# Layer 1's norm weight and bias through the spatial product, plain fp32, and GpSimd's products on VectorE

## The chip, the core and the metric

The kernel runs on one core of a Trainium2 chip: TensorE does matmuls, VectorE and ScalarE elementwise work, GpSimd does elementwise work too, SyncE issues the transfers between HBM and SBUF. The metric is device time in microseconds, the median of several runs. The profile is one execution under the hardware profiler; its times are counted from the span's start.

## The reference

A trunk of two layers on 1024 tokens of width 1024. Layer 0 is a recurrence beside windowed attention and is not touched. Layer 1 is, cut to what matters:

```python
h = rms_norm(x, norm_c[j])
u, v, g = split_cols(h @ w_in_c[j], (2048, 2048, 2048))
v = layer_norm(v, ln_v_g[j], ln_v_b[j])          # (v - mean) * rstd * g + b, over the 2048 columns
# chunks of 128 tokens, 8 groups of 256 columns, W_s lower triangular, one per group
sg = einsum("gts,bcsgd->bctgd", w_s * causal, v) + b_s
y = u * sg * silu(g)
x = x + y @ w_out_c[j]
```

## The kernel before

All products are fp32 in three parts: each operand is split into a high part, a cast to fp32r on ScalarE, and a low part, the difference, made on VectorE, and `mm3` (lines 144 to 147) issues three matmuls. The large products use Winograd's scheme of quarters: seven products in place of eight.

Layer 1 first makes v (lines 956 to 1115) and stores it in HBM (`vdram`) by groups of 256 columns. Then comes the gating stage, lines 1117 to 1328: 8 groups, and in each a gate product and a u product, in this order (`order`, line 1152). Each has seven products of 4 x 3 matmuls of 512 columns (`group_product`, line 1230). After product i it evacuates an accumulator (`done`) and runs the steps listed for i. The order of all engines' work is written out by hand there, and each engine takes its instructions strictly in that order. The steps are these:

- `group_operands` (line 1118) loads the raw weights of the product after next in two tiles (pool of two) and makes, during the running product, the four operands of the next one: sums on GpSimd (`add_up`, line 1134), splits on ScalarE and VectorE (`split`, lines 1141 and 1142), at steps 0 to 3, 5 and 6.
- `group_prep` (line 1195) loads v of the group, its norm weight and bias, the spatial bias and weights, at the start of the gate product; `group_mask` (line 1208, GpSimd) and `group_ws` (line 1212, TensorE transpose and split) run at steps 4 and 5 of it.
- `group_norm` (line 1220) normalizes one token tile of 256 columns of v in two VectorE steps and splits it; its eight calls lie in the steps of the u product.
- `group_u` (line 1259) adds up the quarters of u and multiplies them by the gate, three of four on GpSimd (line 1272).
- `group_spatial` (line 1277) is called four times per group, in steps 0 to 3 of the next gate product: eight matmuls against W's two parts side by side, two additions per bank on VectorE (lines 1292 and 1294), the product with u on GpSimd (line 1295), a store to `ydram`.

An accumulator of a product is reused by a later one: product 3 needs the copy that `done(0)` makes on ScalarE, product 5 that of `done(2)`, product 7 the addition of `done(4)` on VectorE (counted from 1). PSUM has 8 banks that are given out in turn; SBUF has 16 large tiles, of which 14 hold the token operands here and the other two v and the gate of a group.

After the stage the output projection (`winograd`, line 709) loads y back from `ydram` (`load_y`), makes its sums on GpSimd (`combine`, line 748) and splits on ScalarE and VectorE. There the order on ScalarE and VectorE is a planner's.

Of the kernel before, what the change touches and what calls it, by code (L numbers as in the profile page):

```python
# [18 lines left out]
P = 128  # L19
# [8 lines left out]
# the weights to split in a step of mixer B's chunk, by their place in the order of use  # L28
# [8 lines left out]
R_CONV_W, R_CONV_B, R_GAB, R_GXB, R_LAM = 0, 32, 40, 48, 56  # L37
N_ROWS = 64


def bc(ap, pos, n):
    """The access pattern with a repeated dimension of n inserted at pos."""
    dims = [list(d) for d in ap.ap]
    dims.insert(pos, [0, n])
    return bass.AP(tensor=ap.tensor, offset=ap.offset, ap=dims)


def flip(ap):
    """The access pattern with its innermost dimension read backwards."""
# [6 lines left out]
def rows_bc(ap, n):  # L56
    """A DRAM row of n elements, repeated over the partitions."""
    return bass.AP(tensor=ap.tensor, offset=ap.offset, ap=[[0, P], [1, n]])
# [3 lines left out]
def trunk_kernel(  # L62
# [58 lines left out]
    def fetch_weights(i):  # L121
        """Start the loads of the weights up to i, as far as they have not been started."""
# [4 lines left out]
    def load_weights(i, prefetch=True):  # L127
        """Split the weights up to i, as far as they have not been split."""
# [30 lines left out]
    def power_rsqrt(dst, mean, width, name):  # L159
        """dst = (mean + EPS) ** -0.5 on a few columns."""  # L160
# [7 lines left out]
    def norm_rs(xt, t, pool):  # L168
        """The scratch tile of the scaled rows and their reciprocal root mean square."""
# [14 lines left out]
    def h_tiles(tag):  # L184
        """[feature half][token half] tiles of 4 x 512, high and low parts."""
# [24 lines left out]
    # =================== layer 0: norm, keys, values, first gate ===================  # L210
# [35 lines left out]
    # keys of a head: [k; k] stacked over partitions, high and low parts;  # L246
    # values of a block and head: [high | low | high]
# [3 lines left out]
    def kv_pass(t, w_part, h_part, first, last):  # L251
        """One of the three products of parts of the normed rows with the keys' and values' weights."""
# [55 lines left out]
    def load_consts():  # L308
# [3 lines left out]
        for r0, src in ((R_CONV_B, conv_b), (R_GAB, gate_a_b), (R_GXB, gate_x_b), (R_LAM, lru_lambda)):  # L312
            nc.sync.dma_start(out=rows[r0:r0 + 8, :], in_=src[0].rearrange("(k p) -> k p", p=P))
        nc.sync.dma_start(out=rows[R_CONV_W:R_CONV_W + 32, :],
                          in_=conv_w[0].rearrange("w (k p) -> (w k) p", p=P))

    def tail_consts():
        """What is needed later on: the bias by distance, through DRAM for its skewed read, and mixer A's columns."""
# [1088 lines left out]
```

## Time and profile before

| | us |
|---|---|
| median of 3 runs | 1453.38 (1451.16 to 1453.53) |
| span of the profiled execution | 1451.4 |
| TensorE matmuls busy | 1348.5 (93%) |
| VectorE busy | 1111.1 (77%) |
| ScalarE busy | 693.9 (48%) |
| GpSimd busy | 506.3 (35%) |

How to read it: a busy share is an average over stages with different limits, and matmuls overlap in the pipeline, so that a TensorE that is busy is not one without gaps. The distance between the starts of two matmuls says what one costs.

### The profile page before, as it was taken

The page shows a single profiled execution, that of the slowest core. Times are in us where ns is not written, and L with a number is a line of the kernel's source. Part 1 is how long each engine was busy: PE and PEld are TensorE (multiplying, and loading weights), DVE is VectorE, ACT ScalarE, POOL GpSimd, SP SyncE. Part 2 cuts the span into 40 slices and gives each one's busy share as a digit, 9 for nine tenths or more (in the row PEclk, how much of TensorE's full clock was granted, in tenths as well). Part 3 has the DMA queues.
Part 4 walks back from the last instruction along what each step waited for, and adds up shares of the span by engine and source line. Part 5 has one row for each costly group of instructions (what it writes and reads, how often), then busy time and mean ns, then how long its engine had stood idle before and what let it go on. Part 6 is the DMA issues. An engine that isn't in the chain of part 4 may idle for free.

```text
span 1451.4 us, 18932 instructions
## 1 busy us (share of the span) xinstructions
PE 1348.5 (93%) x7003; PEld 1148.9 (79%) x7003; DVE 1111.1 (77%) x1830; ACT 693.9 (48%) x1282; POOL 506.3 (35%) x350
## 2 busy tenths in 40 slices
PE   7999999999999996599998799999988998997998
PEld 6888888888887785488888799777777777775887
DVE  6468888888788889778678745778877887879873
ACT  6467878776777763134423223333333333432430
POOL 3322333221032339300035232444455444488100
PEclk9999999999999998799999899999999999999999
DMA  6212111112211054014412123233223322683321
GB/s 208 59 30 58 29 46 30 44 32 71 58 33 51 4 188 174 16 44 146 159 37 80 68 93 135 65 113 113 91 65 117 109 91 66 216 334 132 113 96 64
DMA packets 100536, 133.53 MB, mean 92 GB/s; under 512 B 5355, under 2 KB 72028, under 8 KB 98396
## 3 DMA queue, kind: packets, MB, share of 16 engines
q1 hardware_dynamic: 100444, 132.32, 27.1%
q8 instruction: 55, 0.90, 0.3%
q14 instruction: 37, 0.30, 0.1%
HBM read 107.11 MB, written 25.19 MB: 91 GB/s over the span
## 4 chain that ended last, share of the span: by engine, by line
PE 59%; DVE 22%; issue 8%; POOL 4%; ACT 4%; DMA 3%; SPq 0%; DVEq 0%; POOLq 0%; ACTq 0%
PE m L145 6%; PE m L146 5%; PE m L147 5%; DVE wlg L1142 3%; PE v L145 3%; PE v L146 3%; PE v L147 3%; DVE wl_w L696 2%; DVE wa L689 2%; PE pq L145 2%; PE gb L145 2%; PE pq L147 2%; PE gb L147 2%; PE pq L146 2%; PE gb L146 2%
## 5 line engine op out<-in xcount | busy, mean ns | idle before, releaser
L145 PE MATMUL m<-wh_w,wa 128*128 128x512 f32 x432 | 170.8, 395 | 34.0 <-DVE x L824 34.0
L146 PE MATMUL m<-wl_w,wa 128*128 128x512 f32 x432 | 170.5, 395 | 4.2 <-DVE wl_w L696 4.2
L147 PE MATMUL m<-wh_w,wa 128*128 128x512 f32 x432 | 170.0, 393 | 0.0
L145 PEld LDWEIGHTS m<-wh_w,wa 128*128 128x128 f32 x432 | 82.3, 190 | 52.9 <-issue 32.8
L146 PEld LDWEIGHTS m<-wl_w,wa 128*128 128x128 f32 x432 | 82.3, 190 | 21.6 <-DVE wl_w L696 5.0
L147 PEld LDWEIGHTS m<-wh_w,wa 128*128 128x128 f32 x432 | 82.3, 190 | 17.3
L1226 ACT CAST vh<-vg 128x256 fp32r<-128x256 f32 x64 | 26.0, 407 | 122.3 <-DVE vg L1224 122.3
L530 DVE CUSTOM_DVE_ANT_0 e<-ps,e,sink_bc 128x256 f32<-128x256 f32 (+1 forms) x128 | 62.3, 525 | 20.6 <-PE ps L527 20.2
L600 POOL TENSOR_TENSOR yb<-ot,yb 128x256 f32<-128x256 f32 x32 | 23.6, 736 | 144.9 <-DVE ot L598 127.2
L134 DVE TENSOR_TENSOR wl<-raw,wh 128x1024 fp32r<-128x1024 f32 x38 | 49.4, 1307 | 26.4 <-ACT wh L133 26.2
L1295 POOL TENSOR_TENSOR ug<-yt,ug 128x512 f32<-128x512 f32 x32 | 41.9, 1319 | 71.5 <-DVE yt L1294 71.4
L696 DVE TENSOR_TENSOR wl_w<-b,wh_w 128x1024 fp32r<-128x1024 f32 x36 | 60.7, 1693 | 6.8 <-ACT wh_w L695 6.8
L545 ACT ACTIVATE e<-e,nm 128x256 f32<-128x256 f32 (+1 forms) x128 | 61.6, 486 | 0.4 <-DVE nm L535 0.4
L695 ACT CAST wh_w<-b 128x1024 fp32r<-128x1024 f32 x36 | 37.5, 1046 | 46.9 <-DVE b L748 22.7
L1272 POOL TENSOR_TENSOR ug<-ug,sg 128x512 f32<-128x512 f32 x24 | 40.7, 1699 | 51.0 <-DVE ug L1271 51.0
L824 DVE TENSOR_TENSOR x<-m,x 128x512 f32<-128x512 f32 x56 | 37.4, 684 | 24.9 <-PE m L147 24.7
L902 POOL TENSOR_TENSOR ya<-ya,r 128x1024 f32<-128x1024 f32 x8 | 22.9, 2859 | 91.2 <-DVE r L898 65.5
L145 PE MATMUL pq<-hh,wh 128*128 128x512 f32 x128 | 52.5, 410 | 0.0
L145 PE MATMUL ga<-hh,wh 128*128 128x512 f32 x128 | 50.3, 393 | 2.2 <-DVE ya L867 2.2
L145 PE MATMUL gb<-hh,wh 128*128 128x512 f32 x128 | 50.3, 393 | 0.0
L145 PE MATMUL za<-hh,wh 128*128 128x512 f32 x128 | 50.2, 392 | 0.0
L147 PE MATMUL pq<-hh,wl 128*128 128x512 f32 x128 | 50.2, 392 | 0.0
(405 smaller groups left out, 4619.0 us busy)
## 6 DMA issues: line engine op xcount, KB each, us to landing
raw<-in_w_in_a_dram SPq DMA_DIRECT2D x34, 512.0 KB, 4.1
b<-in_w_out_a_dram SPq DMA_DIRECT2D x22, 512.0 KB, 6.9
b<-in_w_out_c_dram SPq DMA_DIRECT2D x22, 512.0 KB, 6.0
rawg<-in_w_in_c_dram SPq DMA_DIRECT2D x16, 512.0 KB, 3.6
rawu<-in_w_in_c_dram SPq DMA_DIRECT2D x16, 512.0 KB, 3.7
vg<-vdram SPq DMA_DIRECT2D x8, 1024.0 KB, 5.8
ydram<-ug SPq DMA_DIRECT2D x32, 256.0 KB, 2.4
yg<-ydram SPq DMA_DIRECT2D x8, 1024.0 KB, 10.8
```

Of the source, the lines that this page charges most:

```text
L134: nc.vector.tensor_tensor(out=lo, in0=raws[j], in1=hi.bitcast(F32), op=ALU.subtract)
L145: nc.tensor.matmul(acc, lhsT=lh, rhs=rh, start=first, stop=False, skip_group_check=shared)
L146: nc.tensor.matmul(acc, lhsT=lh, rhs=rl, start=False, stop=False, skip_group_check=shared)
L147: nc.tensor.matmul(acc, lhsT=ll, rhs=rh, start=False, stop=last, skip_group_check=shared)
L530: nc.vector.tensor_tensor_reduce(out=e[:, h, k0:256], in0=acc[:, j * 256:j * 256 + kw], in1=e[:, h, k0:256], scale=rs[:, 2 * (b % 4) + j:2 ...
L545: nc.scalar.activation(out=e[:, h], in_=e[:, h], func=AF.Exp, bias=st["nm"][:, h:h + 1], accum_out=st["sums"][:, h:h + 1])
L695: nc.scalar.copy(out=hi, in_=src)
L696: nc.vector.tensor_tensor(out=lo, in0=src, in1=hi.bitcast(F32), op=ALU.subtract)
L824: nc.vector.tensor_tensor(out=dst, in0=accs[m], in1=dst, op=add)
L1142: nc.vector.tensor_tensor(out=lo[:, j], in0=src, in1=hi[:, j].bitcast(F32), op=ALU.subtract)
L1272: nc.gpsimd.tensor_tensor(out=us[j], in0=us[j], in1=gates[j], op=ALU.mult)
L1295: nc.gpsimd.tensor_tensor(out=ug, in0=y.rearrange("p c t -> p (c t)"), in1=ug, op=ALU.mult)
```

## The change

The layer norm's mean and scale stay with v, as one ScalarE activation per token tile (`rstd` times v plus `shift`). Its weight and bias move behind the spatial product: since that product runs over tokens and the two run over columns, y = weight x (W_s v) + (bias x row sum of W_s + b_s). The last term is `offset`, made once with a matmul of ones. The spatial weights of all groups are loaded, masked and transposed once, in the first gate product. Nothing is split: v and W_s go into TensorE as plain fp32, four matmuls of 128 columns per call in place of eight of 256. One bank per call in place of two, one fused VectorE step in place of four additions. Weight and bias reach the partitions as columns of `cols`, by two more small loads and a longer transpose at the kernel's start. v's tile is read by TensorE itself now, and so the load of the next group's v stands at step 4 of the gate product. The weight sums (`add_up`), the products with the gate and the products with u move from GpSimd to VectorE.

```diff
-R_CONV_W, R_CONV_B, R_GAB, R_GXB, R_LAM = 0, 32, 40, 48, 56
-N_ROWS = 64
+R_CONV_W, R_CONV_B, R_GAB, R_GXB, R_LAM, R_LNG, R_LNB = 0, 32, 40, 48, 56, 64, 80
+N_ROWS = 96
...
         for r0, src in ((R_CONV_B, conv_b), (R_GAB, gate_a_b), (R_GXB, gate_x_b), (R_LAM, lru_lambda)):
             nc.sync.dma_start(out=rows[r0:r0 + 8, :], in_=src[0].rearrange("(k p) -> k p", p=P))
+        for r0, src in ((R_LNG, ln_v_g), (R_LNB, ln_v_b)):
+            nc.sync.dma_start(out=rows[r0:r0 + 16, :], in_=src[0].rearrange("(k p) -> k p", p=P))
         nc.sync.dma_start(out=rows[R_CONV_W:R_CONV_W + 32, :],
                           in_=conv_w[0].rearrange("w (k p) -> (w k) p", p=P))
...
@@ -1131,7 +1133,7 @@
             sums.append(late["vp"].tile([P, 4, P], F32, tag="sum", name=f"s{i}{kind}{g}", bufs=4))
             p, q, op = ((a21, a22, ALU.add), (sums[0], a11, ALU.subtract), (a11, a21, ALU.subtract),
                         (a12, sums[1 % len(sums)], ALU.subtract))[i]
-            nc.gpsimd.tensor_tensor(out=sums[i], in0=p, in1=q, op=op)
+            nc.vector.tensor_tensor(out=sums[i], in0=p, in1=q, op=op)
...
     rstd = const.tile([P, NT], F32, name="rstd")
     for t in range(NT):
         nc.vector.bn_aggr(out=mv[:, t, :], in_=st_all[:, t].rearrange("p a b -> p (a b)"))
+    shift = const.tile([P, NT], F32, name="shift")
     power_rsqrt(rstd, (mv[:, :, 1], 1.0), NT, "lnm")
-    def group_prep(g):
-        v = big_tile(F32, f"vg{g}").rearrange("p (t c) -> p t c", t=NT)
-        nc.sync.dma_start(out=v, in_=vdram[g])
-        lng = gp.tile([P, 256], F32, tag="lng", name=f"lng{g}")
-        lnb = gp.tile([P, 256], F32, tag="lnb", name=f"lnb{g}")
-        sb = gp.tile([P, P], F32, tag="sb", name=f"sb{g}", bufs=2)
-        nc.sync.dma_start(out=lng, in_=rows_bc(ln_v_g[0, g * 256:(g + 1) * 256], 256))
-        nc.sync.dma_start(out=lnb, in_=rows_bc(ln_v_b[0, g * 256:(g + 1) * 256], 256))
-        nc.sync.dma_start(out=sb, in_=rows_bc(spatial_b[0, g], P))
-        ws = gp.tile([P, P], F32, tag="ws", name=f"ws{g}")
-        nc.sync.dma_start(out=ws, in_=spatial_w[0, g])
-        return v, lng, lnb, sb, ws
-    def group_mask(ws):
-        nc.gpsimd.affine_select(out=ws, in_=ws, pattern=[[-1, P]], compare_op=ALU.is_ge, fill=0.0, base=0,
-                                channel_multiplier=1)
-    def group_ws(g, ws):
-        pt = bank(f"pw{g}")
-        nc.tensor.transpose(pt[:, :P], ws, ident)
-        w2 = gp.tile([P, 2, P], F32R, tag="w2", name=f"w2{g}")
-        nc.scalar.copy(out=w2[:, 0, :], in_=pt[:, :P])
-        nc.vector.tensor_tensor(out=w2[:, 1, :], in0=pt[:, :P], in1=w2[:, 0, :].bitcast(F32), op=ALU.subtract)
-        return w2.rearrange("p r t -> p (r t)")
-    def group_norm(t, v, lng, lnb, vh, vl, eng):
-        vv = v[:, t, :]
-        nc.vector.scalar_tensor_tensor(out=vv, in0=vv, scalar=mv[:, t, 0:1], in1=lng,
-                                       op0=ALU.subtract, op1=ALU.mult)
-        nc.vector.scalar_tensor_tensor(out=vv, in0=vv, scalar=rstd[:, t:t + 1], in1=lnb,
-                                       op0=ALU.mult, op1=ALU.add)
-        nc.scalar.copy(out=vh[:, t, :], in_=vv)
-        for i in [t - 1] * (t > 0) + [t] * (t == NT - 1):
-            eng.tensor_tensor(out=vl[:, i, :], in0=v[:, i, :], in1=vh[:, i, :].bitcast(F32), op=ALU.subtract)
+    nc.vector.scalar_tensor_tensor(out=shift, in0=mv[:, :, 0], scalar=-1.0, in1=rstd, op0=ALU.mult, op1=ALU.mult)
+    ws_raw = gp.tile([P, 8, P], F32, name="ws_raw")
+    sb_all = gp.tile([P, 8 * P], F32, name="sb_all")
+    ws_t = gp.tile([P, 8, P], F32, name="ws_t")
+    offset = gp.tile([P, 16, P], F32, name="offset")
+    ones = gp.tile([P, P], F32, name="ones")
+    nc.sync.dma_start(out=ws_raw, in_=spatial_w[0].rearrange("g t s -> t g s"))
+    nc.sync.dma_start(out=sb_all, in_=rows_bc(spatial_b[0, 0], 8 * P))
+    nc.vector.memset(ones, 1.0)
+    def spatial_mask():
+        nc.gpsimd.affine_select(out=ws_raw, in_=ws_raw, pattern=[[0, 8], [-1, P]], compare_op=ALU.is_ge, fill=0.0,
+                                base=0, channel_multiplier=1)
+    def spatial_transpose(i):
+        pt = bank(f"pw{i}")
+        for j in range(4):
+            nc.tensor.transpose(pt[:, j * P:(j + 1) * P], ws_raw[:, 4 * i + j, :], ident)
+        nc.scalar.copy(out=ws_t[:, 4 * i:4 * i + 4, :], in_=pt.rearrange("p (g t) -> p g t", g=4))
+    def spatial_offset(i):
+        pr = bank(f"rw{i}")
+        nc.tensor.matmul(pr, lhsT=ones, rhs=ws_t[:, 4 * i:4 * i + 4, :].rearrange("p g t -> p (g t)"), start=True,
+                         stop=True)
+        for j in range(8):
+            g = 4 * i + j // 2
+            nc.vector.scalar_tensor_tensor(out=offset[:, 8 * i + j, :], in0=pr[:, (j // 2) * P:(j // 2 + 1) * P],
+                                           scalar=col(R_LNB, 8 * i + j), in1=sb_all[:, g * P:(g + 1) * P],
+                                           op0=ALU.mult, op1=ALU.add)
+    vgs = {}
+    def load_v(g):
+        vgs[g] = big_tile(F32, f"vg{g}").rearrange("p (t c) -> p t c", t=NT)
+        nc.sync.dma_start(out=vgs[g], in_=vdram[g])
+    def group_norm(t, g):
+        vv = vgs[g][:, t, :]
+        nc.scalar.activation(out=vv, in_=vv, func=AF.Identity, scale=rstd[:, t:t + 1], bias=shift[:, t:t + 1])
...
                 nc.vector.tensor_tensor(out=us[j], in0=acc, in1=us[j], op=ALU.add)
-                nc.gpsimd.tensor_tensor(out=us[j], in0=us[j], in1=gates[j], op=ALU.mult)
+                nc.vector.tensor_tensor(out=us[j], in0=us[j], in1=gates[j], op=ALU.mult)
...
-    def group_spatial(g, d, half, ug, vhl, w2, sb):
-        vh, vl = vhl
+    def group_spatial(g, d, half, ug):
         y = gp.tile([P, 4, P], F32, tag="yt", name=f"yt{g}_{d}_{half}", bufs=2)
-        avs, yys = [], []
-        for i in range(2):
-            acc = bank(f"s{g}_{d}_{half}_{i}")
-            for j in range(2):
-                ch = half * 4 + i * 2 + j
-                o = acc[:, j * 256:(j + 1) * 256]
-                nc.tensor.matmul(o, lhsT=vh[:, ch, d * P:(d + 1) * P], rhs=w2, start=True, stop=False)
-                nc.tensor.matmul(o, lhsT=vl[:, ch, d * P:(d + 1) * P], rhs=w2, start=False, stop=True)
-            avs.append(acc.rearrange("p (c r t) -> p r c t", c=2, r=2))
-            yys.append(y[:, 2 * i:2 * i + 2, :])
-        for av, yy in zip(avs, yys):
-            nc.vector.tensor_tensor(out=yy, in0=av[:, 0], in1=bc(sb, 1, 2), op=ALU.add)
-        for av, yy in zip(avs, yys):
-            nc.vector.tensor_tensor(out=yy, in0=av[:, 1], in1=yy, op=ALU.add)
-        nc.gpsimd.tensor_tensor(out=ug, in0=y.rearrange("p c t -> p (c t)"), in1=ug, op=ALU.mult)
+        acc = bank(f"s{g}_{d}_{half}")
+        for i in range(4):
+            nc.tensor.matmul(acc[:, i * P:(i + 1) * P], lhsT=vgs[g][:, half * 4 + i, d * P:(d + 1) * P],
+                             rhs=ws_t[:, g, :], start=True, stop=True)
+        nc.vector.scalar_tensor_tensor(out=y, in0=acc.rearrange("p (c t) -> p c t", c=4), scalar=col(R_LNG, 2 * g + d),
+                                       in1=bc(offset[:, 2 * g + d, :], 1, 4), op0=ALU.mult, op1=ALU.add)
+        nc.vector.tensor_tensor(out=ug, in0=y.rearrange("p c t -> p (c t)"), in1=ug, op=ALU.mult)
         nc.sync.dma_start(out=ydram[g, :, d, half * 512:(half + 1) * 512], in_=ug)
...
     spatial = []
+    load_v(0)
     for n, (kind, g) in enumerate(order):
         nxt, steps = following
         if kind == "g":
-            v, lng, lnb, sb, ws = group_prep(g)
-            w2 = []
             for i, args in enumerate(spatial):
                 steps.setdefault(i, []).insert(i > 0, (group_spatial, *args))
-            steps.setdefault(4, []).append((group_mask, ws))
-            steps[5].append((lambda: w2.append(group_ws(g, ws)),))
+            if g == 0:
+                steps.setdefault(2, []).append((spatial_mask,))
+                for i in range(2):
+                    steps.setdefault(4 + i, []).append((spatial_transpose, i))
+            else:
+                steps.setdefault(4, []).append((load_v, g))
             sg = group_gate(g, ops, steps)
         else:
-            vh = gp.tile([P, NT, 256], F32R, tag="vh", name=f"vh{g}")
-            vl = gp.tile([P, NT, 256], F32R, tag="vl", name=f"vl{g}")
             for i in range(8):
-                steps.setdefault(i // 2 if g == 7 else min(i, 6), []).append(
-                    (group_norm, i, v, lng, lnb, vh, vl, nc.gpsimd if g == 7 else nc.vector))
+                steps.setdefault(i // 2 if g == 7 else min(i, 6), []).append((group_norm, i, g))
+            if g == 0:
+                for i in range(2):
+                    steps.setdefault(2 + 2 * i, []).append((spatial_offset, i))
             us = group_u(g, ops, sg, steps)
-            spatial = [(g, d, half, us[2 * d + half], (vh, vl), w2[0], sb)
-                       for d, half in ((0, 0), (0, 1), (1, 1), (1, 0))]
+            spatial = [(g, d, half, us[2 * d + half]) for d, half in ((0, 0), (0, 1), (1, 1), (1, 0))]
```

## Rows read from the trace of the kernel before

**Rows 1.** The page: busy time of the engines, and the chain by engine.

```profile
PE 1348.5 (93%) x7003; PEld 1148.9 (79%) x7003; DVE 1111.1 (77%) x1830; ACT 693.9 (48%) x1282; POOL 506.3 (35%) x350
...
PE 59%; DVE 22%; issue 8%; POOL 4%; ACT 4%; DMA 3%; SPq 0%; DVEq 0%; POOLq 0%; ACTq 0%
```

**Rows 2.** Timeline of TensorE, the gating stage's ends (start, us, instruction).

```profile
898.95 0.40 PE L145 MATMUL g<-gh,whg 128*128 128x512 f32 x1
...
1283.64 0.47 PE L145 MATMUL m<-wh_w,first_c 128*128 128x512 f32 x1 [2.33 <-DVE yt L1294]
```

**Rows 3.** Timeline of TensorE, a stretch without a stop and the stop behind it.

```profile
1068.46 0.39 PE L145 MATMUL u<-t1h,whu 128*128 128x512 f32 x1
...
1073.67 0.39 PE L147 MATMUL u<-t0h,wlu 128*128 128x512 f32 x1
1076.15 0.50 PE L145 MATMUL u<-t2h,whu 128*128 128x512 f32 x1 [2.09 <-ACT ug L1266]
```

**Rows 4.** Timeline of TensorE, one call of the spatial product.

```profile
1087.75 0.28 PE L1287 MATMUL s<-w,vh 128*128 128x256 f32 x1
...
1088.71 0.39 PE L145 MATMUL g<-gh,whg 128*128 128x512 f32 x1
```

**Rows 5.** Waits from 895 to 1290 (total us, times, longest).

```profile
PE u L145 <- ACT ug L1266: 16.2, 11, 2.3
...
PE pw L1214 <- POOL ws L1209: 9.0, 7, 1.3
...
PE m L145 <- DVE yt L1294: 2.3, 1, 2.3
```

**Rows 6.** Timelines of VectorE and ScalarE ahead of the stop in rows 3.

```profile
1069.33 3.01 DVE L1142 TENSOR_TENSOR wlg<-rawg,whg 128x512 fp32r<-128x512 f32 x2
...
1075.21 0.40 ACT L1226 CAST vh<-vg 128x256 fp32r<-128x256 f32 x1 [5.93 <-DVE vg L1224]
1075.52 0.58 ACT L1266 COPY ug<-u 128x512 f32<-128x512 f32 x1
```

**Rows 7.** Groups by line and shape, 930 to 1290 (busy, mean ns).

```profile
L1142 DVE TENSOR_TENSOR wlu<-s0u,whu 128x512 fp32r<-128x512 f32 x7 | 12.4, 1774 | 0.0
...
L1142 DVE TENSOR_TENSOR wlg<-s1g,whg 128x512 fp32r<-128x512 f32 x7 | 4.8, 692 | 8.0 <-ACT whg L1141 8.0
```

**Rows 8.** Busy times (PE, PEld, DVE, ACT, POOL) of 48 us inside the stage.

```profile
1045.00:1093.00 48.00, 43.77 (x201) 35.41 (x201) 38.30 (x63) 16.48 (x33) 22.33 (x16) 1.00 0.28 95
```

**Rows 9.** Transfers by line (KB each, median us from issue to landing).

```profile
rawu<-in_w_in_c_dram SPq DMA_DIRECT2D x16, 512.0 KB, 3.7
vg<-vdram SPq DMA_DIRECT2D x8, 1024.0 KB, 5.8
```

**Rows 10.** fp32 matmuls: two lines (ns min/median/max), and TensorE's timeline around them.

```profile
L484 PE MATMUL st<-pair_ones,sq x128: 171/251/252, 79.2 to 314.8; 128*128 128x2 f32 x128
...
79.22 0.95 PE L484 MATMUL st<-pair_ones,sq 128*128 128x2 f32 x8
80.04 0.48 PE L145 MATMUL pq<-hh,wh 128*128 128x512 f32 x1
...
L320 PE MATMUL pb<-oh,rel_ext x2: 482/488/493, 28.2 to 28.5; 33*16 33x384 f32 x2
...
28.18 0.82 PE L320 MATMUL pb<-oh,rel_ext 33*16 33x384 f32 x2
```

**Rows 11.** A fused VectorE step with a scalar per partition, line 181 (ns min/median/max).

```profile
L181 DVE SCALAR_TENSOR_TENSOR nxs<-xp,nrs,gain_a x10: 744/1270/1285, 8.5 to 40.7; 128x1024 f32<-128x1024 f32 x6, 128x512 f32<-128x512 f32 x4
```

**Rows 12.** Timeline of SyncE's queue: the raw weights' two halves, the second waiting.

```profile
1074.92 15.47 SPq L1125 DMA_DIRECT2D rawu<-in_w_in_c_dram  x2
```

**Rows 13.** Timelines of SyncE's queue and ScalarE at the kernel's start.

```profile
17.89 1.02 SPq L125 DMA_DIRECT2D raw<-in_w_in_a_dram  x2
...
26.58 1.04 ACT L133 CAST wh<-raw 128x1024 fp32r<-128x1024 f32 x1
```

**Rows 14.** Timeline of TensorE in the output projection.

```profile
1334.87 0.77 PE L145 MATMUL m<-wh_w,wa 128*128 128x512 f32 x1 [7.42 <-DVE x L824]
```

## Prediction, before the change was run

> **What bounds the kernel now.** I began with the busy times and the chain of work that ended last [rows 1]: TensorE is busy 93% of the span and carries 59% of the chain, VectorE 22%. That makes TensorE the engine to watch, but not the cause of every microsecond. So I went to the stretch that the change touches, the gating stage, from the first matmul of its first gate product at 898.95 to the first matmul of the output projection at 1283.64 [rows 2]: 384.7 us.
>
> How much of that is work? Between two matmuls of 512 columns without a stop lie (1073.67 - 1068.46) / 23 = 0.2265 us [rows 3]. The stage has 16 products of 7 x 4 x 3 = 84 such matmuls: 1344 x 0.2265 = 304.4. The spatial products are 256 matmuls of 256 columns, eight from 1087.75 to 1088.71, so 0.12 each [rows 4]: 30.7. With eight small transposes, some 0.6 in all, that makes 335.7, so 49.0 us of the stage are not work. That is the most which this stage can give if TensorE's work stays the same.
>
> The list of waits says where the 49.0 are [rows 5]: TensorE waits 16.2 for ScalarE's copy of a u quarter, 9.0 for GpSimd's mask of the spatial weights and 2.3 at the end for VectorE's `yt`: 27.5. The other 21.5 I put down to smaller waits and to what stands right behind each stop (weight loads that wait too, and matmuls that start slower). Who is at the root? One stop read backwards [rows 6]: TensorE stands until 1076.15 [rows 3]; ScalarE's copy began at 1075.52, behind a cast that had waited 5.93 us for VectorE's norm; ahead of that norm VectorE had taken 3.01 us for two subtractions. Undisturbed, such a subtraction takes 0.692 us; of the groups that run beside GpSimd's work one takes 1.774 [rows 7]. So GpSimd's products slow VectorE, VectorE's norm holds ScalarE, and ScalarE holds TensorE. VectorE itself is busy 38.3 of 48 us, GpSimd 22.3 [rows 8].
>
> **The change, part by part.**
>
> *The norm.* Per token tile two VectorE steps, a cast and a subtraction go; one ScalarE activation with scale and bias per partition comes, 64 in all, while 64 casts of 0.40 us go. Nearest row for it: that cast; I take 0.40 and bound it by 0.40 and the 0.58 of a copy of twice the columns [rows 6]. It waits for the load of v alone. That load moves from the start of a gate product to its fifth step, since the tile is now read by the spatial matmuls until the fourth. It issues after TensorE's fourth product and the four stores of `ydram`, by my count 17 us into the product, lands 5.8 us later [rows 9] at 22.8, and is wanted when u's first product is done, near 25.3. If it were over 2.5 us later, ScalarE's queue would hold the copies of u behind it.
>
> *The spatial product in plain fp32.* Eight matmuls become four. The records show two passes for each fp32 matmul: the line of query statistics has 128 for 64 matmuls in the code [rows 10]. Two prices: a pass bound by its weights takes (80.04 - 79.22) / 8 = 0.102; for one bound by streaming, two records of 384 columns that last 0.48 each end 0.82 after the first began, so they start 0.34 apart, 0.88 ns per column, 0.113 for 128 [rows 10]. I take 0.112 as these overlap for other matmuls: 256 passes, 28.7 us in place of 30.7. Bounds: 0.102 (26.1) and load plus stream, 0.215 (55.0). The Trainium skill (FP8 and Floating Point Precision, TensorE Precision Notes) says that a true fp32 product goes through the array four times; with four passes, each with its load, at 0.112 us the 128 matmuls would take 57.3, and the sum below would be 28.6 higher.
>
> *Mask and transposes.* Eight masks and eight transposes inside the loop become one mask and eight transposes in the first gate product: the 9.0 us wait goes. New on TensorE are two fp32 matmuls of 512 columns for the offset: 2 x 2 x 512 x 0.88 ns = 1.8 us, and 8 x 0.11 = 0.9 for the transposes. On VectorE come 16 steps of 128 columns in the first u product, some 4 us (estimate, between a quarter of 0.69 each, 2.8, and the whole, 11), for which it has a third of that product free, some 6 us; what is beyond that stands in the 5 us left over below. The mask is the only GpSimd work; it starts when `ws_raw` has landed, two products ahead of the transposes. The step `shift` makes VectorE wait once for a GpSimd power on 8 columns, while TensorE has 19 us of product ahead; I count nothing.
>
> *GpSimd's products go to VectorE.* Per pair of products (gate and u) VectorE then has 14 subtractions, 8 weight sums, 6 additions, 1 + 3 products with the gate, 4 products with u and 4 fused steps: 36 x 0.69 + 4 x 0.75 = 27.8 us (0.75: the shortest fused step, one of 512 columns [rows 11]). Now it is 38.3 in 48 [rows 8]. Nothing slows it any longer, and the pair shrinks to 38.1 + 3.6 = 41.7 us of TensorE: VectorE would be 67% busy. Queue order matters more: the first weight sum waits in VectorE's queue for the second half of the raw weights, and behind it stand the addition of product 2 and all later ones. These weights are issued when the last split of the product before is done. Now that is late for u (1090.39, 5.4 us into the gate product, as 1074.92 + 15.47; the product began near 1085.0, 12 x 0.2265 ahead of the spatial matmul at 1087.75 [rows 4, 12]); with no backlog I expect 1.8 us, plus 3.7 of transfer [rows 9]: 5.5 us into a product of 19 to 22.6. From there to the addition that product 7 needs lie 11.3 us of VectorE's work in a gate product, done at 16.8; product 7 starts at 19.9. In u it is 7.7 us, or 0.7 us behind product 5; either way before 16.3. So it is covered, by about 2 to 3 us.
>
> *The ends.* Two more small loads stand on SP's queue ahead of the raw weights at 17.89; two issues there take 1.02 us; were it three times that, the weights would issue near 21 and, with 3.7 of transfer, land near 24.7. They are first split at 26.58 [rows 13]: that cover holds, and the cost is 0. Without it, it would be some 1 to 3 us. At the other end the stop of 2.3 us for `yt` goes (already counted), and GpSimd can begin the output projection's sums some 5 us sooner against TensorE, since its products with u no longer stand before them. TensorE stops there once for 7.42 us behind VectorE [rows 14], which GpSimd slows in the same way. I take 2 us, between 0 and 5.
>
> *Sum.* Work after: 304.4 + 28.7 + 0.9 + 1.8 = 335.8. Of the 49.0 I leave 5 (estimate: small losses at 64 changes between the two kinds of products, and the crowded first pair). Stage: 340.8, a gain of 43.9; with the ends 45.9. The profiled execution spans 1451.4 and the median is 1453.4, 2.0 more: 1451.4 - 45.9 + 2.0 = **1407 us**.
>
> **Rivals.** (1) *VectorE late by a little.* It is the only engine for all elementwise steps and strictly in order. If raw weights land 9.6 instead of 5.5 us into a product, the cover of about 3 us is gone and each of the 16 products loses about 1 us: 1407 + 16 = 1423. For it: VectorE's tail is long today and rawu lands near 9.1 us into a gate product (5.4 + 3.7). Against it: that lateness comes from work that is removed.
> (2) *fp32 costs more.* If load and stream of a pass don't overlap, or each matmul has four loaded passes: 55.0 to 57.3 in place of 28.7, so 1407 + 26 to 29, say 1435. Against it: 128 records for 64 matmuls, at 0.102 us each. The Trainium skill's rule of four passes, cited above, would end there.
> (3) *Slower than before.* The same queue, but as a loop: a late last split delays the raw weights, these delay all of VectorE's steps, and these delay the next split. It decides from a landing 11.4 us into every product: 8.6 us is where product 7 begins to wait (19.9 - 11.3, or 16.3 - 7.7), and 44 / 16 = 2.8 us more per product eat the whole gain. At 12.5 us: 1453 + 18 = 1471. For it: a wait for a DMA at the head of the busiest queue. Against it: transfers of 3.6 to 3.7 us and a VectorE with a third of its time free.
> (4) *The gain is given back.* The output projection is short of VectorE; if its stops grow by 8 us, or its order of VectorE's work comes out worse, 1415.
>
> **How the numbers follow.** Forecast 0.62, rival 1 0.17, rival 2 0.10, rival 4 0.05, rival 3 0.06 (of which a third lands near no change). The low end takes the forecast with nothing left of the 49.0, 5 us at the end and the cheap pass: 1407 - 5 - 3 - 2.6, about 1397. The high end takes in rivals 1 and 4 and a few us more: 1427. Out of it stay rivals 2 and 3, 16 in 100. Faster by over 0.2% (what a measurement of this kernel can tell from none): 0.94; within: 0.02; slower: 0.04.
>
> **What would show it.** Right: in the gating stage the pair of groups takes 41.5 to 43 us, TensorE's waits for `ug` and for the mask are gone, the subtractions take 0.69 us throughout, and a spatial product of four matmuls takes 0.9 us. Wrong: a stop ahead of product 7 of each group that names VectorE (rivals 1 and 3), eight passes of far over 0.9 us (rival 2), ScalarE waiting for the load of v at the start of u, or an output projection longer than 1451.4 - 1283.6 = 167.8 us (rival 4).

## The result, and the profile after

| | before | after |
|---|---|---|
| median | 1453.45 us (4 runs, 1451.16 to 1454.42) | 1401.82 us (4 runs, 1400.38 to 1404.61) |
| profiled execution's span | 1451.4 | 1400.7 |
| gating stage | 384.7 | 338.2 |
| output projection of layer 1 | 167.8 | 163.0 |

The ratio (after to before) is 0.9655, 95% interval 0.9640 to 0.9671: 51.6 us faster. The forecast was 1407, in a range of 1397 to 1427.

The page of after, busy times and the chain by engine, against [rows 1]:

```profile
PE 1334.2 (95%) x7007; PEld 1146.0 (82%) x7007; DVE 1021.5 (73%) x1680; ACT 702.2 (50%) x1276; POOL 319.2 (23%) x215
...
PE 74%; DVE 16%; issue 4%; ACT 3%; DMA 2%; POOL 0%; SPq 0%; DVEq 0%; ACTq 0%; POOLq 0%
```

TensorE's share of the chain rises from 59 to 74%, VectorE's falls from 22 to 16%. The timeline of TensorE gives the stage's ends, as in [rows 2], and one call of the spatial product, as in [rows 4]:

```profile
899.51 0.40 PE L145 MATMUL g<-gh,whg 128*128 128x512 f32 x1
...
986.66 1.05 PE L1292 MATMUL s<-ws_t,vg 128*128 128x128 f32 x8
987.47 0.48 PE L145 MATMUL g<-gh,whg 128*128 128x512 f32 x1
...
1237.66 0.48 PE L145 MATMUL m<-wh_w,first_c 128*128 128x512 f32 x1
```

The stage lasts 1237.66 - 899.51 = 338.2 us. A call is eight records for four matmuls, 0.81 us from its first record to the next matmul; by the lengths of the products below it costs 0.91. The waits from 895 to 1240 (total us, times, longest) show one that is left to TensorE:

```profile
PE g L145 <- ACT sg L1258: 1.5, 1, 1.5
...
DVE s0g L1136 <- DMA rawg<-in_w_in_c_dram: 26.8, 7, 4.7
```

The three of [rows 5] are gone. Only the crowded first gate product stops once; VectorE waits for raw weights at the start of products, and nobody waits for VectorE because of it. Groups of after from 940 to 1215 (busy us, mean ns), against [rows 7]:

```profile
L1238 ACT ACTIVATE vg<-vg,shift,rstd 128x256 f32<-128x256 f32 x50 | 28.6, 597 | 0.0
L1144 DVE TENSOR_TENSOR wlu<-rawu,whu 128x512 fp32r<-128x512 f32 x20 | 13.2, 689 | 12.5 <-ACT whu L1143 12.5
```

and a pair of products as a window (busy PE, PEld, DVE, ACT, POOL, then the granted clock), against [rows 8]:

```profile
1022.00:1064.00 42.00, 42.00 (x203) 35.35 (x202) 26.19 (x40) 17.55 (x32) 0.00 (x0) 1.00 0.31 101
```

A pair is a gate product of 22.67 us and a u product of 19.04, 41.7 together, where it was 47 to 49. TensorE has no gap in the window and VectorE is busy 26.2 of 42 us.

### The profile page after: what moved, and what is told of

The parts are those of the page before. It is cut to its first block, busy times and chain, and to the rows that moved or that the text cites. A ratio compares the mean times of both kernels' runs of the same rounds, so it can differ in the third digit from the quotient of the medians.

```text
span 1400.7 us, 18450 instructions
## 1 busy us (share of the span) xinstructions
PE 1334.2 (95%) x7007; PEld 1146.0 (82%) x7007; DVE 1021.5 (73%) x1680; ACT 702.2 (50%) x1276; POOL 319.2 (23%) x215
## 4 chain that ended last, share of the span: by engine, by line
PE 74%; DVE 16%; issue 4%; ACT 3%; DMA 2%; POOL 0%; SPq 0%; DVEq 0%; ACTq 0%; POOLq 0%
PE m L145 4%; PE m L146 4%; PE m L147 4%; PE u L145 4%; PE u L147 4%; PE u L146 4%; PE g L145 3%; PE g L146 3%; PE g L147 3%; DVE wl_w L698 3%; PE v L145 3%; PE v L146 3%; PE v L147 3%; DVE wa L691 3%; PE pq L145 2%
## 5 line engine op out<-in xcount | busy, mean ns | idle before, releaser
L750 POOL TENSOR_TENSOR sa<-yg,yg 128x1024 f32<-128x1024 f32 x4 | 15.7, 3937 | 341.8 <-DVE yt L1294 327.1
L1264 ACT ACTIVATE sg<-sg 128x512 f32<-128x512 f32 x24 | 15.2, 633 | 71.0 <-DVE sg L1263 71.0
L146 PE MATMUL pq<-hl,wh 128*128 128x512 f32 x128 | 50.0, 391 | 0.0
L147 PE MATMUL gb<-hh,wl 128*128 128x512 f32 x128 | 50.0, 391 | 0.0
```

Source lines behind the costliest of these rows:

```text
L146: nc.tensor.matmul(acc, lhsT=lh, rhs=rl, start=False, stop=False, skip_group_check=shared)
L147: nc.tensor.matmul(acc, lhsT=ll, rhs=rh, start=False, stop=last, skip_group_check=shared)
L750: eng.tensor_tensor(out=dst[j], in0=p[j], in1=q[j], op=op)
```

## The experiments

"Stage" below means the distance from the first matmul of the first gate product to the first one of the output projection.

### Which part brings the time

**e1, the products alone.** The kernel before, with GpSimd's sums and products of the stage on VectorE; the masks stay on GpSimd.

```diff
-            nc.gpsimd.tensor_tensor(out=sums[i], in0=p, in1=q, op=op)
+            nc.vector.tensor_tensor(out=sums[i], in0=p, in1=q, op=op)
...
-                nc.gpsimd.tensor_tensor(out=us[j], in0=us[j], in1=gates[j], op=ALU.mult)
+                nc.vector.tensor_tensor(out=us[j], in0=us[j], in1=gates[j], op=ALU.mult)
...
-        nc.gpsimd.tensor_tensor(out=ug, in0=y.rearrange("p c t -> p (c t)"), in1=ug, op=ALU.mult)
+        nc.vector.tensor_tensor(out=ug, in0=y.rearrange("p c t -> p (c t)"), in1=ug, op=ALU.mult)
```

> The kernel before, with one part of the change alone: the weight sums, the products with the gate and with u on VectorE; norm, splits and the spatial product as before. Theory A (the stops come from VectorE's norm, which stands ahead of ScalarE's copies; GpSimd's slowing of VectorE only lengthens it): the sums and products bring VectorE some 10 us of work per pair of products and free it of some 7 us of slowing, so it is busy some 42 us where TensorE needs 42.3, the stops stay in other places, and the time is 1430 to 1455. Theory B (GpSimd's slowing of VectorE is the whole cause): most of the gain is here, under 1420.

Measured: 1456.64 us, ratio 1.0024 (1.0014 to 1.0035), a little slower. The stage takes 383.5 us for 384.7; what is lost lies in the output projection, 172.6 for 167.8. The window of one pair, a long one (the next takes 47.75 us):

```profile
1037.48:1087.96 50.48, 46.39 (x203) 37.78 (x201) 39.90 (x80) 16.54 (x34) 0.69 (x1) 0.93 0.29 92
```

a group, from 1037 to 1230:

```profile
L1142 DVE TENSOR_TENSOR wlu<-s0u,whu 128x512 fp32r<-128x512 f32 x4 | 2.7, 684 | 0.0
```

and the timeline of a stop:

```profile
1077.01 0.42 DVE L1228 TENSOR_TENSOR vl<-vg,vh 128x256 fp32r<-128x256 f32 x1
1077.13 0.41 ACT L1226 CAST vh<-vg 128x256 fp32r<-128x256 f32 x1 [2.60 <-DVE vg L1224]
...
1077.44 0.58 ACT L1266 COPY ug<-u 128x512 f32<-128x512 f32 x1
1078.07 0.50 PE L145 MATMUL u<-t2h,whu 128*128 128x512 f32 x1 [2.01 <-ACT ug L1266]
```

GpSimd is idle but for the mask, and the subtraction that took 1774 ns [rows 7] takes 684. Still VectorE is busy about as long as before, 39.9 of 50.5 us, since it now does the products itself. And the stop has the links of [rows 6]: TensorE behind ScalarE's copy, that behind a cast, that behind VectorE's norm. Over the stage TensorE waits 17.4 us for these copies, where it was 16.2. The 9.0 us for the mask are gone, but the gate products now wait 8.5 for VectorE's addition ahead of product 7, where nothing waited before. So GpSimd's slowing alone was not the root of the stops: it and the work that GpSimd saved VectorE about cancelled.

**e2, the norm alone.** The kernel after, with the three lines of e1 on GpSimd again.

```diff
-            nc.vector.tensor_tensor(out=sums[i], in0=p, in1=q, op=op)
+            nc.gpsimd.tensor_tensor(out=sums[i], in0=p, in1=q, op=op)
...
-                nc.vector.tensor_tensor(out=us[j], in0=us[j], in1=gates[j], op=ALU.mult)
+                nc.gpsimd.tensor_tensor(out=us[j], in0=us[j], in1=gates[j], op=ALU.mult)
...
-        nc.vector.tensor_tensor(out=ug, in0=y.rearrange("p c t -> p (c t)"), in1=ug, op=ALU.mult)
+        nc.gpsimd.tensor_tensor(out=ug, in0=y.rearrange("p c t -> p (c t)"), in1=ug, op=ALU.mult)
```

> The changed kernel with its three GpSimd lines back on GpSimd (weight sums, products with the gate and with u); the norm on ScalarE and the plain fp32 spatial product stay. Theory A: ScalarE no longer waits for VectorE, so the stops for the copies and the mask are gone though VectorE is still slowed: a pair of products takes 41.7 to 43.5 us and the time is 1400 to 1417. Theory B: VectorE's subtractions stay at up to 1.8 us and the stops stay: over 1430.

Measured: 1403.90, ratio 0.9659 (0.9639 to 0.9678). The window of one pair:

```profile
1020.00:1061.70 41.70, 41.70 (x201) 35.11 (x200) 19.78 (x26) 17.65 (x33) 20.16 (x16) 1.00 0.31 101
```

and a group, from 940 to 1215:

```profile
L1144 DVE TENSOR_TENSOR wlg<-s3g,whg 128x512 fp32r<-128x512 f32 x7 | 12.5, 1783 | 0.0
```

The pair is 41.7 us, as in after. A subtraction beside GpSimd's work still takes 1783 ns, and it costs nothing: VectorE has 22 us to spare. The norm, the plain fp32 and the masks together bring nearly the whole gain; the move of GpSimd's products has 2.1 us between the medians, which the intervals do not tell from none.

**e3, only the weight sums on GpSimd, and e4, only the products with gate and u.** Of the diff of e2 the first pair of lines alone, and the other two alone.

> The changed kernel with the weight sums alone back on GpSimd. Theory A: VectorE has a third of its time free, so it makes no difference in the stage: 1399 to 1406, with subtractions of up to 1.8 us again. Theory B: some 1 us per product is lost, 1410 to 1420.

> The changed kernel with the products with the gate and with u alone back on GpSimd. Theory A: no difference in the stage; the output projection may lose the 4.8 us that it gained, if that came from GpSimd being free when the stage ends: 1400 to 1408. Theory B: 1408 to 1420.

Measured: 1404.96, ratio 0.9665 (0.9647 to 0.9684), and 1405.00, 0.9658 (0.9631 to 0.9684). The stage stays within 1 us of that of after in both; the projection takes 166.2 and 166.1 in place of 163.0 us. In e2 it takes 166.1 too.

**e7, only the last group's products on GpSimd.**

```diff
-                nc.vector.tensor_tensor(out=us[j], in0=us[j], in1=gates[j], op=ALU.mult)
+                (nc.gpsimd if g == 7 else nc.vector).tensor_tensor(out=us[j], in0=us[j], in1=gates[j], op=ALU.mult)
...
-        nc.vector.tensor_tensor(out=ug, in0=y.rearrange("p c t -> p (c t)"), in1=ug, op=ALU.mult)
+        (nc.gpsimd if g == 7 else nc.vector).tensor_tensor(out=ug, in0=y.rearrange("p c t -> p (c t)"), in1=ug, op=ALU.mult)
```

> The changed kernel with the products of the last group (gate and u) back on GpSimd. The output projection became 4.8 us shorter with the change. If that is since GpSimd begins its sums earlier: it takes 2 to 5 us longer again, 1404 to 1407. If it came from VectorE's order or from transfers: 1401 to 1403.

Measured: 1404.45, ratio 0.9666 (0.9648 to 0.9684); the projection 166.0. That looks as if GpSimd's last products held up the projection. But e3 has no such products: GpSimd begins the projection's sums there within 0.2 us of the stage's end, as in after, and yet the projection is as long as in e7; in e1 it begins them 1.7 us before the stage's end, and the projection takes 172.6. The traces show what differs. Timelines of GpSimd and VectorE in after:

```profile
1272.04 6.67 POOL L750 TENSOR_TENSOR sa<-yg,yg 128x1024 f32<-128x1024 f32 x1 [6.90 <-DVE wa L691]
...
1274.11 2.34 DVE L698 TENSOR_TENSOR wl_w<-rawc,wh_w 128x1024 fp32r<-128x1024 f32 x2
```

and in e3, with TensorE's stop that follows:

```profile
1272.65 3.26 POOL L750 TENSOR_TENSOR sa<-yg,yg 128x1024 f32<-128x1024 f32 x1 [6.90 <-DVE wa L691]
...
1276.93 6.74 DVE L698 TENSOR_TENSOR wl_w<-rawc,wh_w 128x1024 fp32r<-128x1024 f32 x2
...
1287.69 0.77 PE L145 MATMUL m<-wh_w,wa 128*128 128x512 f32 x1 [5.64 <-DVE x L826]
```

The same steps meet in both. In after GpSimd's sum is held up (6.67 us) and VectorE's two subtractions go through in 2.34; in e3 it is the other way round, 3.26 and 6.74, TensorE stops 5.64 us, and the granted clock behind the stop, from 1287.69 to 1293.20, is 0.50 (in after, from 1287.13 to 1293.00, it is 1.00). The other traces fall in two classes at the same sum, 33 to 34 us into the projection. Where the sum takes 6.7 us (after, e5), the projection is 163.0 and 162.1 long. Where it takes 3.3 (before, e1, e2, e3, e4, e6, e7, e9), TensorE stops there for 5.0 to 10.7 us and the projection is 165.5 to 172.6.

The Trainium skill (SBUF — State Buffer, Who interferes with whom) says that the two engines share a port pair as an exclusive lock, held for the whole instruction by whichever issues first. The exclusive use agrees with the traces: GpSimd's sum takes 2.39 us at its shortest and VectorE's subtraction 1.21, and where they take turns each shows 3.3 to 3.4. The order does not follow from the starts alone: in after the sum that starts at 1272.04 is passed by VectorE steps that start at 1272.97 and 1274.11 (a profile's times on GpSimd are rough).

What decides who goes first here stayed open. The 3 us of the projection are thus not shown to belong to any of the moved lines, and neither are the 4.8 us that it gained with the change: before is of the one class and after of the other.

### Where VectorE's norm costs

**e9, the norm on VectorE.** The kernel after with the norm in two VectorE steps, weight and bias in it; plain fp32 and the rest are kept. Of the edit only the main lines stand below: the offset's matmuls and steps go, and two small loads of weight and bias per group come, ahead of the load of v.

```diff
-        nc.scalar.activation(out=vv, in_=vv, func=AF.Identity, scale=rstd[:, t:t + 1], bias=shift[:, t:t + 1])
+        lng, lnb = lngb[g]
+        nc.vector.scalar_tensor_tensor(out=vv, in0=vv, scalar=mv[:, t, 0:1], in1=lng,
+                                       op0=ALU.subtract, op1=ALU.mult)
+        nc.vector.scalar_tensor_tensor(out=vv, in0=vv, scalar=rstd[:, t:t + 1], in1=lnb,
+                                       op0=ALU.mult, op1=ALU.add)
...
-        nc.vector.scalar_tensor_tensor(out=y, in0=acc.rearrange("p (c t) -> p c t", c=4), scalar=col(R_LNG, 2 * g + d),
-                                       in1=bc(offset[:, 2 * g + d, :], 1, 4), op0=ALU.mult, op1=ALU.add)
+        nc.vector.scalar_tensor_tensor(out=y, in0=acc.rearrange("p (c t) -> p c t", c=4), scalar=1.0,
+                                       in1=bc(sb_all[:, g * P:(g + 1) * P], 1, 4), op0=ALU.mult, op1=ALU.add)
```

> The kernel after, with layer 1's norm back on VectorE in two steps per token tile, weight and bias in it again (64 x 2 steps of 256 columns, 0.48 us each undisturbed in the run with the products alone on VectorE), and nothing on ScalarE for it; the spatial product stays plain fp32. VectorE then has 26.2 + 16 x 0.48 = 33.9 us in a pair of 41.7. Theory 1, what cost time before is that ScalarE's queue stood behind VectorE's norm (the cast of the normed tile) and TensorE behind ScalarE's copies: nothing on ScalarE waits for the norm here, so the pair stays at 41.7 to 42.2 and the time at 1402 to 1408. Theory 2, it is the amount of work on VectorE ahead of the addition that product 7 needs: in the u product that addition ends at 14.5 us now and has up to six more steps of 0.48 ahead of it, 17.4, against 16.3 when product 7 could start, so each u product loses about 1 us and some half clock behind the stop: 1402 + 8 x 1 to 1.5 + g0, 1411 to 1416. If the gain is gone (over 1440), weight and bias had to leave VectorE whatever the splits do.

Measured: 1426.74, ratio 0.9834 (0.9818 to 0.9851): half of the gain is gone, more than either theory said. The timeline of VectorE and TensorE at one u product's stop:

```profile
1068.58 0.48 DVE L1229 SCALAR_TENSOR_TENSOR vg<-vg,mv,lng 128x256 f32<-128x256 f32 x1
1069.09 0.48 DVE L1231 SCALAR_TENSOR_TENSOR vg<-vg,rstd,lnb 128x256 f32<-128x256 f32 x1
1069.49 0.68 DVE L1275 TENSOR_TENSOR ug<-u,ug 128x512 f32<-128x512 f32 x1
...
1070.23 0.50 PE L145 MATMUL u<-t3h,whu 128*128 128x512 f32 x1 [1.69 <-DVE ug L1275]
```

and the window of its pair:

```profile
1029.39:1073.09 43.70, 42.01 (x202) 35.04 (x200) 32.47 (x58) 13.66 (x24) 0.00 (x0) 1.00 0.29 103
```

Theory 1 falls: nothing on ScalarE waits for the norm, and there is a stop. It stands where theory 2 has it: product 7 waits for an addition that stands behind norm steps. VectorE is busy only 32.5 of 43.7 us; its order is what counts.

The gate products are as in after (22.67 to 22.70 us). The u products of groups 1 to 6 take 20.5 to 23.7 in place of 19.0, the last one 24.6 in place of 22.5, and the projection takes 6 us more (TensorE stops 8.68 us at the place told of under e7). The expectation had 1 to 1.5 us per u product, since it counted VectorE's steps alone. But the raw weights land later too: in the two u products looked at, from 962.88 and 1052.06, at 8.2 and 7.5 us in place of 5.7; their first half is issued some 1.4 us later, behind the two loads of weight and bias. Over the u products of groups 0 to 6 the stop grows with this landing: with 5.8 us there is none (the first product, 19.4 us long), with 7.0 it is 1.3 us, with 7.5 1.9, with 8.2 2.5 and with 8.6 2.9. So the norm's steps on VectorE bring the limit down to a landing near 5.7 us, and the later landing then makes the loss; e9 does not tell what the steps would cost without the two loads.

In the three longer u products (22.7 to 23.7 us, stops of 1.9 to 2.9) TensorE's granted clock falls to 0.50 behind the stop, from 983 to 986 for one; in the three shorter ones (20.5 to 21.0, stops of 1.3 to 1.9) it stays at 1.00. The stage takes 356.6 us: with the norm back on VectorE and the rest of the change kept, 28.1 of its 46.5 us are still gained.

### Rival 3, the loop

**e5 and e6, each load of raw weights issued twice, and three times.**

```diff
-            nc.sync.dma_start(out=raw[kh], in_=w_in_c[kh * 512:(kh + 1) * 512, c0:c0 + 256].rearrange("(k p) c -> p k c", p=P))
+            for _ in range(2):
+                nc.sync.dma_start(out=raw[kh], in_=w_in_c[kh * 512:(kh + 1) * 512, c0:c0 + 256].rearrange("(k p) c -> p k c", p=P))
```

> The changed kernel with each load of raw gate and u weights issued twice into the same tile, which delays the point from which VectorE may add them. By the prediction's third rival TensorE begins to wait at product 7 when the weights land 8.6 us into a product; from the trace of the changed kernel I now read 8 to 9.5. Two transfers in a row land near 9 us: a loss of 0 to 1 us per product, 1402 to 1420. If the queue order of VectorE doesn't matter: 1402, also with three transfers.

> The same with three transfers in a row, landing near 13 us into a product, beyond the 11.4 us from which the third rival says that the whole gain is gone: 4 us and more lost per product, 1455 to 1490, with TensorE waiting for VectorE ahead of product 7 or later ones. If the queue order of VectorE doesn't matter: 1402.

Measured: 1464.47, ratio 1.0090 (1.0075 to 1.0105), and 1560.85, 1.0747 (1.0726 to 1.0769). Both lie far above what was expected, since the weights land later than either expectation had it: a later copy waits for the one before into the same tile, so that in a u product of e5 the whole set lands not at 5.7 us, nor near the 9 expected, but at 15.3. The timeline of e5's u product that begins at 1076.39:

```profile
1091.66 0.62 ACT L1144 CAST whg<-rawg 128x512 fp32r<-128x512 f32 x1 [4.44 <-DMA rawg<-in_w_in_c_dram]
1091.66 0.69 DVE L1137 TENSOR_TENSOR s0g<-rawg,rawg 128x512 f32<-128x512 f32 x1 [13.24 <-DMA rawg<-in_w_in_c_dram]
...
1092.68 0.56 ACT L1277 COPY ug<-u 128x512 f32<-128x512 f32 x1
...
1093.30 0.80 PE L145 MATMUL u<-t2h,whu 128*128 128x512 f32 x1 [5.87 <-ACT ug L1277]
```

and of its gate product that begins at 1052.31:

```profile
1073.49 0.51 PE L145 MATMUL g<-t3h,whg 128*128 128x512 f32 x1 [1.08 <-DVE sg L1264]
```

In the gate product the weights land 9.4 us in, and product 7 starts 1.23 us late behind VectorE's addition: the wait begins at a landing near 8.2, where the prediction said 8.6. In the u product it is another engine: ScalarE's cast of the raw weights waits, and behind it in ScalarE's queue stands the copy that product 5 needs. Product 5 starts 6.0 us late at a landing of 15.3, so there the limit is 9.2. The second thing is the clock behind the stop, in a window:

```profile
1093.30:1096.50 3.20, 3.20 (x8) 2.53 (x9) 3.17 (x6) 3.15 (x7) 0.00 (x0) 0.50 0.00 0
```

TensorE stood 6 us and then ran 3.2 us at a granted clock of 0.50 (1.2 of 2.4 GHz): eight matmuls 0.43 apart in place of 0.2265, another 1.6 us. In e6 a gate product waits for ScalarE at product 5 too (2.95 us at 1111.03), and the u product behind it for 11.40. The mean landing in e5 is (9.4 + 15.3) / 2 = 12.35 us, and the time 13 us above before; the prediction had 18 at 12.5. So late weights do cost more than the whole gain, as rival 3 has it, and its price comes out near. In part that is luck: the rival spread the loss evenly and put it on VectorE ahead of product 7, and measured it is some 1.5 us in most gate products and some 6.6 in a u product, there behind ScalarE. The loop itself, in which a late last split keeps the weights late, was not tried: here they are late by the number of loads. What kept the change out of this is that its landings stay at 5.2 to 5.7.

### A version that beats both

The waits of after's layer 0 hold one of 26.1 us that no line of the change touches: the output projection there, built by the same function.

**e8, the projections' sums on VectorE.** After, with the four token sums of both output projections moved from GpSimd, and **e10**, the same edit in the kernel before.

```diff
-                combine(nc.gpsimd, xs[n], a21, a22, add)
+                combine(nc.vector, xs[n], a21, a22, add)
...
-                combine(nc.gpsimd, a21, a11, a21, sub)
-                combine(nc.gpsimd, a11, xs[n], a11, sub)
+                combine(nc.vector, a21, a11, a21, sub)
+                combine(nc.vector, a11, xs[n], a11, sub)
...
-                combine(nc.gpsimd, a12, a12, a11, sub)
+                combine(nc.vector, a12, a12, a11, sub)
```

> The changed kernel with the sums of the token operand in both output projections on VectorE too (four lines), the same move as in the gating stage. VectorE is busy 34.2 of 35 us there and its steps take up to 3.4 us beside GpSimd, 1.2 alone. If the slowing is what costs: 5 to 15 us less, 1387 to 1397. If VectorE's own work is what costs: some 39 us more on VectorE in two stretches that have none to spare, 1405 to 1425.

> The kernel before, with the token sums of both output projections on VectorE in place of GpSimd and nothing else changed. On the kernel after this move gave 24.5 us: 22.2 in layer 0's projection, 3.8 in layer 1's. If it is independent of the change, layer 0's projection again takes about 150 in place of 172 us, layer 1's 167.8 less what GpSimd's last products with u had held up, and the time is 1453.4 - 22 to 28 = 1425 to 1431. If it needs the change (VectorE's order, GpSimd free at the stage's end), layer 1's part is below 2 us and the time 1430 to 1433, or no better than before in layer 1.

Measured: e8 1377.33, ratio to before 0.9489 (0.9474 to 0.9503), 24.5 us below after where 5 to 15 were expected. e10 1419.87, ratio 0.9787 (0.9772 to 0.9802), 31.4 us below before and more than expected. Layer 0's projection in after, the stop in TensorE's timeline:

```profile
596.61 0.76 PE L145 MATMUL m<-wh_w,wa 128*128 128x512 f32 x1 [26.09 <-DVE x L826]
```

the window around it:

```profile
560.00:600.00 40.00, 13.91 (x55) 11.07 (x54) 40.00 (x19) 8.08 (x8) 31.28 (x10) 0.68 0.27 92
```

and a group, from 521 to 695:

```profile
L698 DVE TENSOR_TENSOR wl_w<-b,wh_w 128x1024 fp32r<-128x1024 f32 x18 | 32.6, 1822 | 0.5 <-ACT wh_w L697 0.5
```

In e8 the same window:

```profile
560.00:600.00 40.00, 37.73 (x163) 29.97 (x162) 39.87 (x40) 15.45 (x16) 0.00 (x0) 1.00 0.35 117
```

and the same group:

```profile
L698 DVE TENSOR_TENSOR wl_w<-b,wh_w 128x1024 fp32r<-128x1024 f32 x18 | 21.9, 1220 | 0.4 <-ACT wh_w L697 0.4
```

VectorE is busy for 40 us in both windows, but does 19 instructions in the one and 40 in the other; the mean subtraction falls from 1822 to 1220 ns, and the projection (up to the first transpose behind it) from 172.2 to 150.0 us. Here VectorE is the engine that bounds, and here GpSimd's slowing is the root: the same reading that e1 refuted in the gating stage. e10's layer 1 projection takes 157.8 us for 167.8, so in before it had 10 us to lose, and 159.3 in e8. That the change's 4.8 us there are a part of these 10 is likely, but not shown.

## Why the prediction was right, point by point

**The bound and the size of the gain: right.** The stage came out at 338.2 us for 340.8. The distances between the starts of TensorE's some 1610 matmul records in the stage, less 0.2265, 0.12 or 0.11 by their columns, show what the 49.0 of before were: 36 stops (over 0.28 us each) with 39.1, 15 matmuls of 512 columns that took 0.12 to 0.28 longer with 2.9, and 6.7 in small amounts. After, the same count gives 2.5, 0.4 and 0.9, of which 0.8 are the offset's fp32 matmuls, that is work. By the prediction's own sum 338.2 - 335.8 = 2.4 of the 5 us left over came, 1.7 of it in the one stop of the first gate product. More than half of the 21.5 beside the three waits, 39.1 - 27.5 = 11.6, lay in stops too.

**The root: wrong in one link.** "GpSimd's products slow VectorE, VectorE's norm holds ScalarE, and ScalarE holds TensorE." The last two links stand in e1's stop as in [rows 6]; the first is refuted there: without GpSimd's products TensorE waits as long for ScalarE's copies (17.4 us for 16.2). e2 shows the reverse, slowing without stops. What failed is that I took a lengthened step for its cause, and did not set GpSimd's help against its harm: the 15 products and sums of a pair that it takes from VectorE are 15 x 0.69 = 10 us, about as much as it slowed the rest. The sum did not suffer, since the change removes the norm as well; that was luck, for by the same reading the products alone would have been worth a gain, and e1 measured none.

**The norm: activation mis-sized.** It takes 0.597 us, not 0.40, and outside the bound of 0.58. The nearest row was a cast with no operand per partition. The Trainium skill (ScalarE: Activation LUTs, What ACT_TABLE_LOAD costs) gives 186 ns, 0.833 ns per column and about 93 for each operand per partition: an estimate by it, for 256 columns and two operands, is 585 ns. The trace agrees (597 ns), and that page would have been the better price. It cost nothing here, as ScalarE is busy 17.6 of 42 us. The load of v is issued 18.1 us into the gate product (17 predicted) and takes 6.6 us (5.8), so it lands at 24.7; the first activation that reads it begins 3.4 us into u, 26.1 from the gate product's start. The cover held, by 1.4 us.

**Plain fp32: right.** Gate products are 22.67 - 19.04 = 3.63 us longer than u products; over 32 passes that is 0.113, where 0.112 was taken. Rival 2 falls: two records per matmul, each as long as a pass that is bound by streaming, and the weight load adds nothing. A matmul of 128 columns thus takes 0.227 us, 1.77 ns per column, which is four times the 0.2265 / 512 = 0.44 ns of the split products. The rule of four passes (the Trainium skill, FP8 and Floating Point Precision, TensorE Precision Notes) agrees with that, if a record holds two of the four. What was wrong is the price that rival 2 gave the rule, four passes at 0.112 us each; by rows alone, four at 0.44 ns x 128 are 0.227.

**Mask, transposes, offset: right.** The offset's matmuls make the first u product 20.84 - 19.04 = 1.8 us longer; its 16 VectorE steps take 4.3 us (4 estimated) and stop nobody.

**The queue order: right.** Raw weights were said to land 5.5 us into a product; the first sum that needs them starts 5.7 into u and 5.2 into the gate product. Product 7's addition is done 18.2 us into the gate product, 16.8 predicted, and product 7 starts at 19.95. So the cover is 1.7 rather than 2 to 3 us, and e5 puts the limit at 8.2.

**The ends: right in sign, small.** At the start the first gate product begins 0.6 us later, 0 predicted; in e2, e3, e4, e7 and e9, which have the new start too, it begins between 0.8 earlier and 1.2 later than in before, so that is scatter. The projection gained 4.8, not 2, inside the 0 to 5; but the reason that I gave, GpSimd's earlier sums, does not hold: e3 has them as early and takes 166.2 us, and e1 has them earlier and takes 172.6. What differs is who goes first at one sum (e7 above), so this term came out near by luck.

**The sum.** -46.5 in the stage, -4.8 in the projection and +0.6 ahead make -50.7, where the prediction had -45.9. The 4.8 between them are 2.6 of the stage, a leftover taken too large, and 2.2 of the ends, taken too small; the median lies 1.1 above the span, where 2.0 was added.

## What to carry to other kernels

An engine whose steps are slowed by a neighbour is at the root of a stop only if it is short of time there. Count what the neighbour saves it as well as what it costs, and look at whether it is busy all through the window (layer 0's projection, 40 of 40 us) or only late in its order (the gating stage). In a strict queue the price of a step is set by what stands behind it: take the steps out from ahead of the one instruction that the busiest engine waits for. And look at the loads that an edit puts ahead of others in the queue of transfers: in e9 two small ones came, and the weights behind them landed 1.3 to 2.9 us later in most u products.

## What the runs showed of the hardware

After a stop of 6 us TensorE ran 3.2 us at a granted clock of 0.50, with matmuls of 512 columns 0.43 us apart (e5). In e9 the clock fell to 0.50 behind stops of 1.9, 2.5 and 2.9 us and stayed at 1.00 behind others of 1.3 to 2.0; in e1, with stops of at most 3 us, the mean clock of one pair is 0.93. A stop can thus cost more than its own length.

Where VectorE and GpSimd worked side by side in an output projection, a 128x1024 subtraction lasted 3.4 us in place of 1.2, or GpSimd's sum 6.67 in place of 2.39. Which of them lost changed between kernels that differ only in steps of the gating stage (after and e3).
